# Wider additions of sums, and one more pair of k tiles by seven products, in an encoder block on one core

## The chip, the cores and the metric

The kernel runs on one core of a Trainium2 chip. The metric is the device time of one execution in microseconds (us). A core has TensorE (PE; its weight loads are shown apart as PEld), VectorE (DVE), ScalarE (ACT), GpSimd (POOL) and SyncE (SP). SyncE and GpSimd issue the transfers between the chip's memory and the core's own memory, each on a queue of its own, and sixteen DMA engines carry them out.

## The reference

One layer of a bidirectional encoder for 256 tokens of 2048 features, all in float32:

```python
proj = rmsnorm(h, mix_norm_pre) @ w_in                 # 2048 -> 4640
z, xbc, dt_raw, u = split(proj)
mix = concat([ssd_mixer(z, xbc, dt_raw, ...), pool_mixer(u, ...)]) @ w_out
h = h + rmsnorm(mix, mix_norm_post)
up = rmsnorm(h, ffn_norm_pre) @ w_ffn_up               # 2048 -> 2 x 5632
gate, val = split(up, 2)
ff = (gelu(dwconv_centred(gate, ...)) * val) @ w_ffn_down   # 5632 -> 2048
h = h + rmsnorm(ff, ffn_norm_post)
gate = sigmoid(rmsnorm(h, ple_norm_pre) @ w_ple_gate)  # 2048 -> 2048
h = h + rmsnorm(gate * (p @ w_ple), ple_norm_post)
```

What costs time are the matrix products: w_in, w_out, up, down and the gate. The change touches three of them.

## The kernel before

**Split numbers.** Every product is done three times, in a faster rounded format (fp32r). A factor x is split into hi, x rounded by ScalarE (`split`, line 196, or `hid_split`, line 1369), and lo, the rest x - hi, a subtraction on VectorE (lines 197 and 1370). Then x @ w is hi @ hi + hi @ lo + lo @ hi. So each weight costs ScalarE one pass and VectorE one pass before TensorE can use it. The split weights lie in five buffers (tag `w`); a ScalarE pass waits until TensorE has left the buffer.

**Pairs of k tiles.** In w_out, down and the gate (`token_major`), the columns come in two halves of 1024, and the rows of the weights in pairs of k tiles of 128 rows each. A plain pair is 2 k tiles x 2 token tiles x 2 column blocks of 512 x 3 = 24 matmuls of 512 columns. A pair can instead be done by seven products (`seven_products`, Strassen's scheme in Winograd's form), which is 7 x 3 = 21 matmuls. It needs four sums of blocks of the weights (`block_adds`, line 305) and four sums of blocks of the left factor (`pair_sums`, lines 1202 to 1207, and in `cat_sums` for w_out). Its weights are split in four pieces, named a (512 columns), b, d and c (1024 each), against two pieces of 1024 for a plain pair. d and c are made from the block sums. `combine` puts the products together once per half.

**Where sums are made.** Block sums of down and the gate are mostly made early, in the up stage, and stored: `block_sums` loads 1 MB of weights (`fetch`, tile dnb or gtb), adds (`add`) and stores them in the chip's memory (`store`, on GpSimd's queue, tile dns or gts). A list `which` holds them; the two for the first pairs of down stay in the core's memory. Job number i is placed at up's piece 45 i / 10 + 4, its additions three pieces later. Pairs listed in `dn_here` (15 in the first half; 6 and 13 in the second) make their block sums in down itself, just before the pair. The left factor of down, the hidden activations, has its sums stored in up for the pairs in `dn_stored` (tile hsum, 512 KB each), kept in place for `OWN`, and loaded again by GpSimd (line 1521, tile hd, three buffers).

**Down's second half.** Pairs are numbered 0 to 21; pair u holds the k tiles 2u and 2u + 1. Tiles are named by half and k tile: dn120 is the pair of k = 20 in the second half, that is pair 10. With r ends the name of the weights as loaded (three buffers), with t that of the block sums, with aw to dw that of the split pieces; weights of plain pairs appear as dn1r, dn_0w and dn_1w. `dn_fast` lists the pairs done by seven products. In the second half the plain pairs are 0, 1, 10, 17, 20 and 21. A fast pair with stored block sums loads 768 KB of weights and 1024 KB of sums; a plain pair loads 1024 KB. SyncE's loads for this half are chained in program order (`load`, `IN_ORDER`). The first weights of the gate (tile gtf, 1 MB, `first_raw`) are asked for ahead of pair 13 and aren't chained.

**The order of work.** Up to w_out, and in up, ScalarE, VectorE and SyncE keep the order of the program (`in_order`). In down and the gate a planner orders each engine's instructions when the program is built, by its own costs, within the data's dependencies.

Of the kernel before, what the change touches and what calls it, by code (L numbers as in the profile page):

```python
# [86 lines left out]
def build(nc, a, out):  # L87
    x = a["x"][0]
# [5 lines left out]
    with tile.TileContext(nc) as tc, \  # L94
# [29 lines left out]


        ep = early.enter_context(tc.tile_pool(name="early", bufs=1))
        mhalf = cp.tile([P, 44], F32, name="mhalf")
        nc.gpsimd.memset(mhalf, -0.5)
        ident = cp.tile([P, P], F32, name="ident")
        make_identity(nc, ident)  # L130

# [74 lines left out]
        class Panel:  # L206
# [58 lines left out]
        def block_sums(name, w, c0, k, held):  # L265


            pg = []

            def fetch():  # L270
                r = page(f"{name}b{c0}_{k}")
                pg.append(r)
                load(r, w[c0 // 1024, k // 2])

            def add():
                add_blocks(pg[0])
# [23 lines left out]
        def block_adds(r, t=None):  # L300

            v = r.rearrange("p (b c) -> p b c", b=4)
            s = v if t is None else t.rearrange("p (b c) -> p b c", b=4)
            for n, (i, a, b) in enumerate(((1, v, 0), (0, v, 3), (3, s, 1), (2, s, 3))):
                nc.vector.tensor_add(s[:, i], v[:, i], a[:, b])  # L305
                if n == 1:
                    yield

        def add_blocks(r, t=None):
            for _ in block_adds(r, t):  # L310
                pass
# [182 lines left out]
        for u in range(0, NK, 2):  # L494
            r = [wp.tile([P, 2048], F32, tag="raw", bufs=3, name=f"dtur{u}") if u else r0, page(f"dtur{u + 1}")]
            for j in range(2):
                k = u + j
# [20 lines left out]
            for j in range(2):  # L518
                k = u + j
# [139 lines left out]
                                        1.0 - 2.0 * d, None, op0=ALU.mult)  # L659
            done.add("steps")  # L660

        pth = cp.tile([P, 2, L], F32R, name="pth")
        ptl = cp.tile([P, 2, L], F32R, name="ptl")

        def embedding():

# [372 lines left out]

        sums_got, sums_pages = {}, []  # L1040

        def cat_sums(k):
            if k < 8:
                yield from after(f"yt{k}")
            else:
                yield from after(f"map{(k - 8) // 2}")
            yield from take("mid")
            n = len(sums_got)
            sums_got[k] = None
            if n % 2 == 0:  # L1050
# [6 lines left out]
            a11, a21, a12, a22 = (v[:, i * P:(i + 1) * P] for i in range(4))  # L1057
            s1, s2, s3, s4 = (s[:, i * P:(i + 1) * P] for i in range(4))
            nc.vector.tensor_sub(s1, a22, a21)
            nc.vector.tensor_sub(s3, a11, a21)  # L1060
            nc.vector.tensor_add(s2, s1, a11)
            nc.vector.tensor_sub(s4, a12, s2)
            yield
            nc.scalar.copy(o[:, :512], s[:, :512])
            yield
            nc.vector.tensor_sub(o[:, 512:], s[:, :512], o[:, :512].bitcast(F32))
            give("mid")
            sums_got[k] = {f"s{i + 1}": (o[:, i * P:(i + 1) * P], o[:, 512 + i * P:512 + (i + 1) * P]) for i in range(4)}
# [86 lines left out]
        def turn_over():  # L1155
            go_on()
            next_piece()
            go_on()

        jobs = dict(fill=seg_fill, h=load_h, piled=piled, gate=gate, yturn=y_turn, csum=cat_sums, steps=steps, mix_in=pool_mix, map=pool_map, sums=seg_sums, decays=decays, seg=seg, cb=cb,  # L1160
                    weigh=weigh, turn=xs_turn, far=far, skip=skip, mix=mix, embedding=embedding)

        with in_order():
            for _ in range(AHEAD - 2):
                next_piece()
            for n in range(24):
                slab, i, q = (2, 0, 1)[n // 8], n // 4 % 2, n % 4
# [27 lines left out]
            load(g, src.partition_broadcast(P))  # L1195
            return g

        def pair_sums(name, s, o, a11, a21, a12, a22):


            s1, s2, s3, s4 = (s[:, i * P:(i + 1) * P] for i in range(4))
            nc.vector.tensor_sub(s1, a22, a21)
            nc.vector.tensor_sub(s3, a11, a21)
            nc.vector.tensor_add(s2, s1, a11)
            nc.vector.tensor_sub(s4, a12, s2)  # L1205
            nc.scalar.copy(o[:, :512], s[:, :512])  # L1206
            nc.vector.tensor_sub(o[:, 512:], s[:, :512], o[:, :512].bitcast(F32))
            return sums_in(o)

        def sums_in(o):  # L1210
            return {f"s{i + 1}": (o[:, i * P:(i + 1) * P], o[:, 512 + i * P:512 + (i + 1) * P]) for i in range(4)}

        class Sums:
# [5 lines left out]
            def __call__(self, k):  # L1219
                if k not in self.got:  # L1220
                    n = len(self.got)
                    if n % 2 == 0:
                        self.pages.append(page(f"{self.name}p{k}", F32R))
                    s = mid(f"{self.name}s{k}")
                    c = slice((k % 8) * L, (k % 8 + 2) * L)
                    v = s[:, 512:]
                    nc.vector.tensor_add(v, self.pan.hi[k // 8][:, c].bitcast(F32), self.pan.lo[k // 8][:, c].bitcast(F32))
                    self.got[k] = pair_sums(f"{self.name}{k}", s, self.pages[-1][:, n % 2 * 1024:(n % 2 + 1) * 1024],
                                            *(v[:, i * P:(i + 1) * P] for i in range(4)))
# [110 lines left out]
            h_kept.append(dp.tile([P, D], F32, tag=f"h{t}", bufs=1, name=f"h_kept{t}"))  # L1340
        pl_kept = dp.tile([P, D], F32, tag="pl", bufs=1, name="pl_kept")

        dn_fast, gt_fast = ((1,2,3,4,5,6,7,8,9,10,11,12,13,14,15,16,17,18,19), (2,3,4,5,6,7,8,9,11,12,13,14,15,16,18,19)), ((4, 5, 6), (1, 2, 3))

        dn_here = (15,), (6,13,)
        dn_stored = (2,3,5,7,8,10,11,13,14,16,17,18,19)
# [7 lines left out]
        jobs_at[6].append(lambda: load(pl_kept, pl[0]))  # L1354
        for i, w_ in enumerate(which[2:] + which[:2]):
            fetch, add, store = block_sums(*w_, i >= len(which) - 2)
            n = 45 * i // 10 + 4
            jobs_at[n].append(fetch)
            jobs_at[n + 3].extend((add, store))
        hid, kept = [], {}  # L1360

        def hid_part(k):
            return hid[k // 8][:, (k % 8) * L:(k % 8 + 2) * L]
# [10 lines left out]
            early_hs[k] = hid_split(k)  # L1374

        def hid_sums_of(k, s, o):
            return pair_sums(f"he{k}", s, o, *(hid_part(k)[:, i * P:(i + 1) * P] for i in (2, 3, 0, 1)))

        OWN = (12, 18, 24, 30)
        own, own_pages = {}, []  # L1380
# [13 lines left out]
        def own_sums(k):  # L1394
            own[k] = hid_sums_of(k, sp.tile([P, 512], F32, tag="junk", bufs=1, name=f"hs{k}"), own_place(k))
# [72 lines left out]
        with in_order():  # L1468
# [3 lines left out]
            for n in range(NPIECES):  # L1472
                s, v, i = blocks[n // 4]
# [98 lines left out]
        vg = [page(f"vg{t}") for t in range(2)]  # L1572
        sq = [[], []]

        half_up = cp.tile([P, 1], F32, name="half_up")
        nc.gpsimd.memset(half_up, 0.5)

        def rest_of(o):

            base = EPS * D  # L1580
            for n, q in enumerate(sq[1]):
                m = tiny(f"go1m{n}", 1)
                nc.gpsimd.tensor_scalar(m, q, 1.0, base, op0=ALU.mult, op1=ALU.add)
                base = m
            nc.gpsimd.tensor_tensor(o, m, half_up, op=ALU.pow)

        def finish(t):
            if t:
# [20 lines left out]
        for half in range(2):  # L1609
# [127 lines left out]
```

## Time and profile before

| what | value |
|---|---|
| median of three runs | 1097.18 us (1096.76 to 1097.2) |
| profiled execution | 1096.73 us, span 1095.0 us |
| TensorE busy | 1088.7 us, 99% of the span |
| VectorE busy | 976.5 us, 89% |
| ScalarE busy | 738.2 us, 67% |
| transfers | 367.45 MB, 336 GB/s over the span |
| stages, by first matmul | xbc 52, z 137, w_out 190, up 285, down 777, gate 1000 us |

The span runs from the first to the last instruction; the profiled execution's own time holds a little more around it. A line such as `L305 DVE TENSOR_TENSOR dnb<-dnb 128x512` names the kernel's line, the engine, the operation, the tiles written and read, and the shape. All matmuls have line 123, that of a helper, so they are told apart by tiles: dna, dns, dn0s and dn1s are the accumulators of down, ga and va those of up. In a timeline the columns are start and duration in us, and in square brackets the idle time before and what ended it.

### The profile page before, as it was taken

The page shows a single profiled execution, that of the slowest core. Times are in us where ns is not written, and L with a number is a line of the kernel's source. Part 1 is how long each engine was busy: PE and PEld are TensorE (multiplying, and loading weights), DVE is VectorE, ACT ScalarE, POOL GpSimd, SP SyncE. Part 2 cuts the span into 40 slices and gives each one's busy share as a digit, 9 for nine tenths or more (in the row PEclk, how much of TensorE's full clock was granted, in tenths as well). Part 3 has the DMA queues.
Part 4 walks back from the last instruction along what each step waited for, and adds up shares of the span by engine and source line. Part 5 has one row for each costly group of instructions (what it writes and reads, how often), then busy time and mean ns, then how long its engine had stood idle before and what let it go on. Part 6 is the DMA issues. An engine that isn't in the chain of part 4 may idle for free.

```text
span 1095.0 us, 15720 instructions
## 1 busy us (share of the span) xinstructions
PE 1088.7 (99%) x5766; PEld 937.1 (86%) x5766; DVE 976.5 (89%) x1367; ACT 738.2 (67%) x1109; POOL 100.1 (9%) x163
## 2 busy tenths in 40 slices
PE   9999999999999999999999999999999999999998
PEld 9988888888888888888888888888888888888886
DVE  6678988999879888889889988888999999999997
ACT  6687777566776565565756646657688868786773
POOL 0211111100100000000000000000000000051001
PEclk9999999999999999999999999999999999999999
DMA  9987699587589999989999998999999999996872
GB/s 359 426 250 203 202 278 279 212 317 273 189 346 404 398 402 364 398 345 373 389 364 378 369 386 349 408 357 423 366 409 382 380 346 390 424 390 221 320 278 78
DMA packets 59565, 367.45 MB, mean 336 GB/s; under 512 B 6672, under 2 KB 7696, under 8 KB 24208
## 3 DMA queue, kind: packets, MB, share of 16 engines
q1 hardware_dynamic: 45808, 302.74, 70.5%
q0 software_dynamic: 13536, 63.44, 17.3%
q8 instruction: 45, 0.74, 0.3%
q14 instruction: 32, 0.26, 0.1%
q10 hardware_dynamic: 144, 0.26, 0.1%
HBM read 315.56 MB, written 61.34 MB: 344 GB/s over the span
## 4 chain that ended last, share of the span: by engine, by line
PE 97%; DVE 1%; POOL 1%; ACT 0%; issue 0%; POOLq 0%; DVEq 0%; ACTq 0%
PE ga L123 22%; PE va L123 22%; PE dna L123 11%; PE xbc L123 6%; PE woa L123 5%; PE gt L123 5%; PE dns L123 4%; PE dtu L123 4%; PE z L123 4%; PE dn0s L123 2%; PE dn1s L123 2%; PE ple L123 1%; PE wo1s L123 1%; PE gts L123 1%; PE yd L123 1%; PE pw L123 1%
## 5 line engine op out<-in xcount | busy, mean ns | idle before, releaser
L123 PE MATMUL ga<-wox,ug_0w 128*128 128x512 f32 x704 | 130.8, 337 | 0.0
L123 PE MATMUL ga<-wox,ug_1w 128*128 128x512 f32 x704 | 130.1, 337 | 0.0
L123 PE MATMUL va<-wox,uv_0w 128*128 128x512 f32 x704 | 129.2, 336 | 0.0
L123 PE MATMUL va<-wox,uv_1w 128*128 128x512 f32 x704 | 129.2, 336 | 0.0
L123 PEld LDWEIGHTS ga<-wox,ug_0w 128*128 128x128 f32 x704 | 107.7, 188 | 14.5 <-ACT pl L1289 0.2
L123 PEld LDWEIGHTS ga<-wox,ug_1w 128*128 128x128 f32 x704 | 107.5, 188 | 14.5 <-DVE wox L234 0.2
L123 PEld LDWEIGHTS va<-wox,uv_1w 128*128 128x128 f32 x704 | 107.5, 188 | 14.5
L123 PEld LDWEIGHTS va<-wox,uv_0w 128*128 128x128 f32 x704 | 107.5, 188 | 14.5
L305 DVE TENSOR_TENSOR dnb<-dnb 128x512 f32<-128x512 f32 x128 | 88.3, 690 | 3.0
L283 POOL DMA_DIRECT2D dns<-dnb x30 | 16.1, 536 | 317.4 <-DVE dnb L305 256.2
L1206 ACT CAST he<-he 128x512 fp32r<-128x512 f32 x13 | 8.1, 621 | 42.8 <-DVE he L1205 42.8
L123 PE MATMUL xbc<-hn,xb_1w 128*128 128x512 f32 x192 | 36.5, 338 | 0.0
L123 PE MATMUL xbc<-hn,xb_0w 128*128 128x512 f32 (+1 forms) x192 | 36.4, 340 | 0.0
L123 PEld LDWEIGHTS xbc<-hn,xb_0w 128*128 128x128 f32 x192 | 29.7, 188 | 4.1
L123 PEld LDWEIGHTS xbc<-hn,xb_1w 128*128 128x128 f32 x192 | 29.5, 188 | 4.1 <-issue 0.2
L1369 ACT CAST hs<-hid 128x384 fp32r<-128x384 f32 (+1 forms) x44 | 23.5, 538 | 12.9 <-PE dna L123 12.7
L1449 ACT ACTIVATE fc<-gr,vt 128x256 f32<-128x256 f32 x44 | 26.1, 593 | 8.6 <-DVE gr L1442 8.6
L1521 POOL DMA_DIRECT2D hd<-hsum x24 | 12.7, 529 | 191.0 <-PE dn1s L123 76.3
L123 PE MATMUL dna<-dn_0w,hs 128*128 128x512 f32 x108 | 28.3, 391 | 0.0
L123 PE MATMUL dna<-dn_1w,hs 128*128 128x512 f32 x108 | 28.0, 390 | 0.0
L1370 DVE TENSOR_TENSOR hs<-hid,hs 128x384 fp32r<-128x384 f32 (+1 forms) x44 | 25.5, 582 | 2.1 <-ACT hs L1369 2.1
L1452 DVE TENSOR_TENSOR fc<-fc,ft 128x510 f32<-128x510 f32 x22 | 15.2, 689 | 11.3 <-ACT ft L1450 11.3
(1778 smaller groups left out, 2796.0 us busy)
## 6 DMA issues: line engine op xcount, KB each, us to landing
dnb<-w_down SPq DMA_DIRECT2D x32, 1024.0 KB, 10.4
dns<-dnb POOLq DMA_DIRECT2D x30, 1024.0 KB, 7.0
hd<-hsum POOLq DMA_DIRECT2D x24, 512.0 KB, 8.1
dtur<-w_dtu SPq DMA_DIRECT2D x14, 528.0 KB, 9.6
hsum<-he POOLq DMA_DIRECT2D x13, 512.0 KB, 7.8
gtb<-w_gate SPq DMA_DIRECT2D x6, 1024.0 KB, 10.1
gts<-gtb POOLq DMA_DIRECT2D x6, 1024.0 KB, 9.2
dn1r<-w_down SPq DMA_DIRECT2D x6, 1024.0 KB, 6.8
```

Of the source, the lines that this page charges most:

```text
L123: last["pe"] = ins(nc.tensor.matmul(o, lhsT, rhs, start=start, stop=stop, skip_group_check=True))
L283: nc.gpsimd.dma_start(t, pg[0])
L305: nc.vector.tensor_add(s[:, i], v[:, i], a[:, b])
L1206: nc.scalar.copy(o[:, :512], s[:, :512])
L1369: nc.scalar.copy(t[:, :c1], hid_part(k)[:, :c1])
L1370: nc.vector.tensor_sub(t[:, 512:512 + c1], hid_part(k)[:, :c1], t[:, :c1].bitcast(F32))
L1449: nc.scalar.activation(c[:, f], v[:, f], AF.Identity, bias=vec(V_FCB + 4 * s + 2 * i + f), scale=vec(w + NF))
L1452: nc.vector.tensor_add(c[:, :, 1:], c[:, :, 1:], l[:, :, :L - 1])
L1521: nc.gpsimd.dma_start(o.bitcast(F32), kept[k])
```

## The change

Four things change.

1. In `block_adds` the first two of the four additions of 128 x 512 become one of 128 x 1024, with blocks taken in reversed order and with a stride of three blocks. The third and fourth stay.
2. The four sums of the left factor get one helper, `four_sums`. Its first two subtractions of 128 x 128 become one of 128 x 256, one operand being read twice. It is used in w_out, down and the gate.
3. Pair 10 of down's second half (k = 20) is done by seven products. Its block sums are one more job in up, so the list has 39 jobs instead of 38, and job i is placed at piece 44 i / 10 + 4. Its hidden sums are in `dn_stored` already, for the first half; the second half loads them once more.
4. Some small tiles change size or place: `mhalf` has 32 columns instead of 44, `half_up` 24 instead of 1, and `pth` and `ptl` (the split embedding) are allocated earlier. The work done on them is the same.

```diff
@@ build
-        mhalf = cp.tile([P, 44], F32, name="mhalf")
+        mhalf = cp.tile([P, 32], F32, name="mhalf")
         nc.gpsimd.memset(mhalf, -0.5)
+        pth = cp.tile([P, 2, L], F32R, name="pth")
+        ptl = cp.tile([P, 2, L], F32R, name="ptl")
...
@@ block_adds
-            for n, (i, a, b) in enumerate(((1, v, 0), (0, v, 3), (3, s, 1), (2, s, 3))):
-                nc.vector.tensor_add(s[:, i], v[:, i], a[:, b])
-                if n == 1:
-                    yield
+            nc.vector.tensor_add(s[:, 1::-1], v[:, 1::-1], v[:, 0::3])
+            yield
+            nc.vector.tensor_add(s[:, 3], v[:, 3], s[:, 1])
+            nc.vector.tensor_add(s[:, 2], v[:, 2], s[:, 3])
...
+        def four_sums(s, v, diagonal, a21, a12):
+
+            s, v = (x.rearrange("p (i c) -> p i c", i=4) for x in (s[:, :512], v))
+            nc.vector.tensor_sub(s[:, 2::-2], v[:, diagonal], v[:, a21].unsqueeze(1).to_broadcast([P, 2, P]))
+            nc.vector.tensor_add(s[:, 1], s[:, 0], v[:, diagonal.start])
+            nc.vector.tensor_sub(s[:, 3], v[:, a12], s[:, 1])
...
@@ cat_sums (and the same in pair_sums)
-            nc.vector.tensor_sub(s1, a22, a21)
-            nc.vector.tensor_sub(s3, a11, a21)
-            nc.vector.tensor_add(s2, s1, a11)
-            nc.vector.tensor_sub(s4, a12, s2)
+            four_sums(s, v, slice(0, 4, 3), 1, 2)
...
@@ pairs of down and the gate
-        dn_fast, gt_fast = ((1,2,3,4,5,6,7,8,9,10,11,12,13,14,15,16,17,18,19), (2,3,4,5,6,7,8,9,11,12,13,14,15,16,18,19)), ((4, 5, 6), (1, 2, 3))
+        dn_fast, gt_fast = ((1,2,3,4,5,6,7,8,9,10,11,12,13,14,15,16,17,18,19), (2,3,4,5,6,7,8,9,10,11,12,13,14,15,16,18,19)), ((4, 5, 6), (1, 2, 3))
...
-            n = 45 * i // 10 + 4
+            n = 44 * i // 10 + 4
...
-        half_up = cp.tile([P, 1], F32, name="half_up")
+        half_up = cp.tile([P, 24], F32, name="half_up")
```

More of the change, by code (lines that the diff above doesn't have):

```diff
@@ L660, in steps @@
             done.add("steps")
-        pth = cp.tile([P, 2, L], F32R, name="pth")
-        ptl = cp.tile([P, 2, L], F32R, name="ptl")
         def embedding():
@@ L1056, in cat_sums @@
             nc.vector.tensor_add(v, cat.hi[k // 8][:, c].bitcast(F32), cat.lo[k // 8][:, c].bitcast(F32))
-            a11, a21, a12, a22 = (v[:, i * P:(i + 1) * P] for i in range(4))
-            s1, s2, s3, s4 = (s[:, i * P:(i + 1) * P] for i in range(4))
-            nc.vector.tensor_sub(s1, a22, a21)
-            nc.vector.tensor_sub(s3, a11, a21)
-            nc.vector.tensor_add(s2, s1, a11)
-            nc.vector.tensor_sub(s4, a12, s2)
+            four_sums(s, v, slice(0, 4, 3), 1, 2)
             yield
@@ L1196, in gload, with pair_sums @@
             return g
[L1198 to L1205, printed above, removed]
+        def pair_sums(s, o, v, *places):
+            four_sums(s, v, *places)
             nc.scalar.copy(o[:, :512], s[:, :512])
@@ L1227, in __call__ @@
                     nc.vector.tensor_add(v, self.pan.hi[k // 8][:, c].bitcast(F32), self.pan.lo[k // 8][:, c].bitcast(F32))
-                    self.got[k] = pair_sums(f"{self.name}{k}", s, self.pages[-1][:, n % 2 * 1024:(n % 2 + 1) * 1024],
-                                            *(v[:, i * P:(i + 1) * P] for i in range(4)))
+                    self.got[k] = pair_sums(s, self.pages[-1][:, n % 2 * 1024:(n % 2 + 1) * 1024], v, slice(0, 4, 3), 1, 2)
                 (h1, l1), (h2, l2) = self.pan(k), self.pan(k + 1)
@@ L1376, in hid_sums_of @@
         def hid_sums_of(k, s, o):
-            return pair_sums(f"he{k}", s, o, *(hid_part(k)[:, i * P:(i + 1) * P] for i in (2, 3, 0, 1)))
+            return pair_sums(s, o, hid_part(k), slice(2, 0, -1), 3, 0)
         OWN = (12, 18, 24, 30)
@@ L1584, in rest_of @@
                 base = m
-            nc.gpsimd.tensor_tensor(o, m, half_up, op=ALU.pow)
+            nc.gpsimd.tensor_tensor(o, m, half_up[:, :1], op=ALU.pow)
         def finish(t):
```

## The prediction

> **What bounds the kernel now.** I read the page first, then the chain of waits, then windows over the stretch where the new pair goes, then the timelines of the engines and queues in it.
>
> ```profile
> span 1095.0 us, 15720 instructions
> PE 1088.7 (99%) x5766; PEld 937.1 (86%) x5766; DVE 976.5 (89%) x1367; ACT 738.2 (67%) x1109; POOL 100.1 (9%) x163
> PE 97%; DVE 1%; POOL 1%; ACT 0%; issue 0%; POOLq 0%; DVEq 0%; ACTq 0%
> ```
>
> The profiled execution took 1096.73 us (its span of 1095.0 and 1.73 around it), 0.45 under the median of the runs, 1097.18. TensorE is the chain, so what counts is what else is full where the change touches it. In the chain of waits:
>
> ```profile
> 732.42 22.19 PE ga L123 x128
> 933.19 5.44 PE dna L123 x24
> 939.31 2.04 PE dna L123 x9
> 944.07 2.04 PE dna L123 x9
> 953.67 2.04 PE dna L123 x9
> ```
>
> A half slab of up is 128 matmuls in 22.19 us. In down, the plain pair k = 20 (the one to be changed) is 24 matmuls in 5.44; from 939.31 to 944.07 a pair by seven products, 21 matmuls, takes 4.76. The next two take 9.60 instead of 9.52: TensorE hardly waits. Then windows; the last three columns are granted clock, DMA share and GB/s.
>
> ```profile
> 100.00:200.00 100.00, 100.00 (x521) 84.30 (x520) 92.09 (x143) 71.31 (x143) 11.48 (x17) 1.00 0.80 245
> 500.00:600.00 100.00, 100.00 (x579) 88.12 (x578) 89.56 (x132) 58.51 (x88) 5.85 (x11) 1.00 0.96 375
> 905.32:910.08 4.76, 4.76 (x22) 3.94 (x21) 4.76 (x7) 4.20 (x6) 0.53 (x1) 1.00 0.99 350
> 919.00:944.00 25.00, 25.00 (x112) 20.68 (x111) 23.00 (x26) 18.93 (x24) 1.07 (x3) 1.00 1.01 411
> 924.36:929.12 4.76, 4.76 (x22) 3.94 (x22) 4.76 (x7) 3.72 (x4) 0.53 (x2) 1.00 0.99 373
> 938.64:943.40 4.76, 4.76 (x22) 3.94 (x22) 3.83 (x5) 4.51 (x6) 0.00 (x0) 1.00 1.00 424
> ```
>
> In up VectorE (the third busy time) has 10 of 100 us free. From 919 to 944 TensorE has no idle time, VectorE has 2 of 25 us, and the DMA engines are always busy (share 1.01, 411 GB/s). Three full resources meet where the change adds work to one and bytes to another.
>
> **The change: TensorE.** One pair goes from 24 to 21 matmuls: 5.44 - 4.76 = 0.68 us less. This is all that it can win on the chain directly.
>
> **The change: VectorE.** Its timeline around the plain pair, and at the next pair whose block sums are made in down (k = 26):
>
> ```profile
> 928.91 1.22 DVE L197 TENSOR_TENSOR dn118cw<-dn118t,dn118cw 128x1024 fp32r<-128x1024 f32 x1
> 930.05 1.22 DVE L197 TENSOR_TENSOR dn_0w<-dn1r,dn_0w 128x1024 fp32r<-128x1024 f32 x1
> 944.75 1.29 DVE L305 TENSOR_TENSOR dn126t<-dn126r 128x512 f32<-128x512 f32 x2
> 945.96 0.69 DVE L305 TENSOR_TENSOR dn126t<-dn126r,dn126t 128x512 f32<-128x512 f32 x1
> 946.56 0.69 DVE L197 TENSOR_TENSOR dn126aw<-dn126r,dn126aw 128x512 fp32r<-128x512 f32 x1
> 947.76 1.22 DVE L197 TENSOR_TENSOR dn126bw<-dn126r,dn126bw 128x1024 fp32r<-128x1024 f32 x1
> 948.90 0.56 DVE L1370 TENSOR_TENSOR hs<-hid,hs 128x384 fp32r<-128x384 f32 x1
> 949.37 1.22 DVE L197 TENSOR_TENSOR dn126dw<-dn126t,dn126dw 128x1024 fp32r<-128x1024 f32 x1
> ```
>
> What one instruction costs the engine is the step to the next start: 1.14 for 1024 columns (928.91 to 930.05), 0.60 for 512 (945.96 to 946.56), 0.47 for 384 (948.90 to 949.37). A plain pair is 2 x 1.14 + 0.60 = 2.88; a pair by seven products with stored sums is 0.60 + 3 x 1.14 + 0.47 = 4.49. So k = 20 adds 1.61, and TensorE asks for everything behind it 0.68 sooner: 2.29 us of slack are wanted. From 930.05 to 944.75 VectorE has 14.70 us and works 2.88 (k = 20) + 2 x 4.02 (the weights of k = 22 and 24) + 3 x 0.47 (three hidden splits) = 12.33. It has 2.37 to spare, so VectorE alone just bears it.
>
> The wider block addition: two instructions of 512 columns become one of 1024, 1.20 to 1.14, 0.06 less. No such form with two strided inputs stands in the trace; the bounds are 1.14 and two whole durations of the 512 form, 1.38 (0.18 more). I take the lower, since the nearest row, a two-input subtraction of 1024 columns, has it. The wider 128-column subtractions:
>
> ```profile
> 892.46 0.28 DVE L1202 TENSOR_TENSOR hs<-hid 128x128 f32<-128x128 f32 x1
> 892.66 0.28 DVE L1203 TENSOR_TENSOR hs<-hid 128x128 f32<-128x128 f32 x1
> ```
>
> Two steps of 0.20 become one of 256 columns, between 0.20 and 0.40; some 0.07 less each. Most of these sums lie in up, z and w_out, under matmuls that run on; I count 0 for them, with 0.1 either way.
>
> **The change: up.** One job more: a load and a store of 1 MB each, and 1.14 + 2 x 0.60 = 2.34 us of additions. Against it stand 38 jobs that save 0.06 (2.3 us) and the narrow sums. VectorE's free 10% hides both, and TensorE's 22.19 shows that its weights were never late. The DMA share goes from 0.96 to about 0.97, the spacing of jobs from 4.5 to 4.4 pieces. I count 0. Were that cover gone, it would cost at most the 2 MB at 411 GB/s, 5 us; nothing in the chain over up speaks for it.
>
> **The change: DMA in down.** Here the bill comes. The loads in order, on SyncE's queue and (hd) on GpSimd's:
>
> ```profile
> 918.94 0.33 SPq L152 DMA_DIRECT2D dn1r<-w_down  x1
> 928.75 0.44 SPq L152 DMA_DIRECT2D gtf<-w_gate  x1
> 932.43 0.33 SPq L152 DMA_DIRECT2D dn126r<-w_down  x1
> 928.73 0.53 POOL L1521 DMA_DIRECT2D hd<-hsum  x1 [4.23 <-PE dn1s L123]
> 943.98 0.53 POOL L1521 DMA_DIRECT2D hd<-hsum  x1 [14.73 <-PE dn1s L123]
> DMA to landing us min/median/max: 11.7/11.7/11.7
> DMA to landing us min/median/max: 12.9/12.9/12.9
> 944.22 0.63 ACT L196 CAST dn126aw<-dn126r 128x512 fp32r<-128x512 f32 x1 [0.83 <-DMA dn126r<-w_down]
> 962.41 1.05 ACT L196 CAST gtfh<-gtf 128x1024 fp32r<-128x1024 f32 x1
> dn122r<-w_down SPq DMA_DIRECT2D x1, 768.0 KB, 7.3
> dn1r<-w_down SPq DMA_DIRECT2D x1, 1024.0 KB, 8.6
> hd<-hsum POOLq DMA_DIRECT2D x3, 512.0 KB, 8.3
> ```
>
> dn126r (11.7 from issue to landing) lands at 932.43 + 11.7 = 944.1, behind gtf (12.9) at 928.75 + 12.9 = 941.7: 1 MB in 2.45 us, back to back. It is already just in time: ScalarE waits for it until 944.22, and VectorE's additions start at 944.75. The plain pair's 1024 KB, issued at 918.94, become 768 KB of weights and 1024 KB of stored block sums, 768 KB more on SyncE's queue ahead of dn122r, dn124, gtf and dn126r, which all wait behind it. The stored hidden sums of k = 20 are one more load of 512 KB on GpSimd. These loads are released by the third one before them, so k = 28's, now issued at 928.73, moves to the end of the new pair, about 938, and runs beside gtf and dn126r.
>
> At 411 GB/s, 768 KB (0.786 MB) is 1.9 us and 512 KB (0.524 MB) is 1.3: an upper bound of 3.2. The lower bound is the first alone at 424 GB/s, 1.9, less what the slow window at 924 could still move ((424 - 373) x 4.76 = 0.24 MB, 0.6): 1.3. I take 2.2, as part of the second will be over by then. dn126r then lands at 946.3 and the additions start at 946.4 instead of 944.75: 1.65 late, 1.59 after the wide one.
>
> Is there slack behind it? TensorE at this pair, the window behind it, and a row of the chain that the sum below uses:
>
> ```profile
> 948.66 0.39 PE L123 MATMUL dna<-dn126bw,hs 128*128 128x512 f32 x1
> 944.75:971.90 27.15, 27.15 (x120) 22.27 (x120) 27.15 (x32) 21.98 (x28) 14.31 (x3) 1.00 1.01 418
> 914.56 2.27 PE dna L123 x9
> ```
>
> dn126bw's subtraction begins at 947.76 and needs 1.22, to 948.98; its first matmul is issued at 948.66, while it ends. There is none. From 944.75 to 971.90, past the plain pair k = 34, VectorE has no pause (27.15 of 27.15), so TensorE follows it 1.59 later than now, and the 0.68 it had won is spent in the wait (about 2.3 us in all). What follows k = 34 is as before, shifted.
>
> **Sum.** -0.68 won, +2.27 waited at k = 26, and 0.06 won at each of the two other pairs with sums made in down (k = 30 of the first half, k = 12 of the second, where TensorE waits today: 2.27 for nine matmuls at 914.56 instead of 2.04): about +1.5 us. 1096.73 + 1.5 = 1098.2 for a profiled execution, **1098.6** as a median. With the bounds of the delay, 1.3 to 3.2, the wait leaves +0.6 to +2.5, which is 1097.7 to 1099.6.
>
> **Rivals.**
> - *The bytes find room (about 1096.3).* gtf is first read at 962.41 and isn't chained to the other loads. If the planner puts it behind dn126r, that load comes 2.45 earlier, at 946.3 - 2.45 = 943.9, before VectorE is ready at 944.75 - 0.68 = 944.07. Then all of 0.68 + 3 x 0.06 = 0.86 is won. For it: the load is free to move. Against it: its issue stands right behind dn124's, and nothing in the diff moves it.
> - *The queue runs at its slow rate (about 1100.1, slower by over 0.2%).* At the 350 GB/s of the window at 905, also at share 0.99 and beside a hidden-sums load, 1.31 MB take 3.7 us: dn126r lands at 947.8, +3.1 - 0.1 = +3.0. It decides from a delay of about 2.9 on, where the loss passes 2.2 us. For it: two such windows lie close by. Against it: gtf to dn126r moved 1 MB in 2.45 us, 428 GB/s. [...]
> - *The wide addition is no gain (+0.5).* With 1.38 for it, each of the three pairs made in down costs 0.18 more instead of 0.06 less, 0.7 in all: 1099.3, if the wait at k = 26 stands.
> - *Something before down moves by over 2 us* (another order of instructions in z and w_out, where VectorE is 92% busy, or in the gate): 1094 to 1096. The edits there are five sums and one block addition, so little speaks for it.
>
> **How the numbers follow.** What a measurement of this kernel can tell from no change is about 0.2%, 2.2 us. Forecast 0.57, room 0.19, slow queue 0.12, no gain 0.06, elsewhere 0.06. Faster by over 0.2%: the last and a little of the second, 0.07. Slower: the slow queue, the top of the forecast's range and of the fourth case, 0.19. Within: 0.74. The range runs from just under the first rival to the slow queue: 1096.0 to 1100.2.
>
> **What would show it.** Right: ScalarE and VectorE wait for the DMA of dn126r by 1.5 us or more; dn126r lands near 946.3; TensorE's gaps at k = 26 add up to about 2.3 us, with none at k = 20 to 24; up's half slabs still take 22.19. Wrong: gtf issued behind dn126r; no gap at k = 26; a 1024-column addition far from 1.22 us long; gaps in up.

## The result, and the profile after

The changed kernel takes 1101.1 us (median of 7 runs, 1100.37 to 1102.44) against 1097.2 for the kernel before on the same chip (7 runs, 1096.76 to 1098.16): a ratio of 1.0034, with a 95% interval of 1.0024 to 1.0044. It is slower by 3.9 us, where the prediction had 1098.6 and a range up to 1100.2. The profiled execution took 1102.24 us, 5.5 more than that of before; some of this difference is one of the execution and not of the kernel, as will be seen.

From the page of the changed kernel, engines, the chain's shares and the block additions that are left in up:

```profile
span 1100.5 us, 15662 instructions
PE 1091.4 (99%) x5763; PEld 938.0 (85%) x5763; DVE 975.0 (89%) x1303; ACT 739.6 (67%) x1111; POOL 101.0 (9%) x165
...
PE 89%; DVE 5%; issue 1%; DMA 1%; ACT 1%; POOL 1%; POOLq 0%; DVEq 0%; ACTq 0%
...
L306 DVE TENSOR_TENSOR dnb<-dnb 128x1024 f32<-128x1024 f32 x33 | 40.2, 1218 | 0.3 <-DMA dnb<-w_down 0.3
```

TensorE has its three matmuls less, VectorE has less to do than before (975.0 instead of 976.5), and a wide addition takes the 1.22 us that was assumed. Yet TensorE's share of the chain fell from 97% to 89%: other engines now end last. Where, the chain of waits shows (start, duration, what):

```profile
732.69 22.19 PE ga L123 x128
...
932.58 1.15 DVE dn120bw L199
933.75 15.37 DMA dn126r<-w_down
949.14 1.23 DVE dn126t L306
...
952.75 2.55 PE dna L123 x5
```

Up's half slab still takes 22.19. Then the load of dn126r stands in the chain, and behind it VectorE's additions, before TensorE goes on. The timelines of VectorE, ScalarE and TensorE at this place (in brackets the idle time before, and what ended it):

```profile
949.14 1.23 DVE L306 TENSOR_TENSOR dn126t<-dn126r 128x1024 f32<-128x1024 f32 x1 [1.85 <-DMA dn126r<-w_down]
...
952.62 0.68 DVE L309 TENSOR_TENSOR dn126t<-dn126r,dn126t 128x512 f32<-128x512 f32 x1
...
949.19 0.62 ACT L198 CAST dn126aw<-dn126r 128x512 fp32r<-128x512 f32 x1 [2.50 <-DMA dn126r<-w_down]
...
953.41 1.04 ACT L198 CAST dn126dw<-dn126t 128x1024 fp32r<-128x1024 f32 x1 [2.66 <-DVE dn126t L309]
...
953.77 1.05 PE L123 MATMUL dna<-dn126bw,hd 128*128 128x512 f32 x2
954.63 0.68 PE L123 MATMUL dna<-dn126dw,hs 128*128 128x512 f32 x1
```

Three things are to be seen. Both engines wait for dn126r, by 1.85 and 2.50 us. The rounding of dn126d starts 953.41 - 949.14 = 4.27 us after the additions began. Before, they began at 944.75 (in the prediction), and VectorE's last addition and ScalarE's rounding were

```profile
947.16 0.69 DVE L305 TENSOR_TENSOR dn126t<-dn126r,dn126t 128x512 f32<-128x512 f32 x1
...
947.96 1.06 ACT L196 CAST dn126dw<-dn126t 128x1024 fp32r<-128x1024 f32 x1 [1.75 <-DVE dn126t L305]
```

which is 947.96 - 944.75 = 3.21. And two matmuls of 512 columns take 954.63 - 953.77 = 0.86 us, 0.43 each, where they took 2.04 / 9 = 0.227 before. Windows over the same place explain the last (the third column from the end is the granted clock):

```profile
948.00:950.00 2.00, 1.00 (x5) 0.52 (x3) 0.86 (x1) 0.81 (x2) 0.00 (x0) 1.00 1.00 418
950.00:952.00 2.00, 1.55 (x5) 0.72 (x5) 2.00 (x4) 0.76 (x1) 0.00 (x0) 1.00 1.03 428
952.00:954.00 2.00, 1.25 (x3) 1.05 (x4) 1.30 (x2) 0.59 (x1) 0.00 (x0) 0.65 1.02 428
954.00:956.00 2.00, 2.00 (x5) 1.10 (x5) 1.51 (x2) 2.00 (x4) 0.00 (x0) 0.50 1.01 414
956.00:958.00 2.00, 2.00 (x10) 1.64 (x9) 2.00 (x3) 2.00 (x3) 0.00 (x0) 1.00 1.02 409
```

After two windows with TensorE partly idle, its clock was halved for 3.4 us: (1 - 0.65) / 0.5 x 2 = 1.4 us of the third window and all of the fourth.

Not all of the time is lost at k = 26. SyncE's queue is a clock of progress: each load is released by the work a few pairs earlier. Before:

```profile
749.66 0.42 SPq L152 DMA_DIRECT2D dnb<-w_down  x1
...
763.34 0.33 SPq L152 DMA_DIRECT2D dn06t<-dns  x1
...
833.07 0.33 SPq L152 DMA_DIRECT2D dn030r<-w_down  x1
...
898.50 0.33 SPq L152 DMA_DIRECT2D dn112r<-w_down  x1
```

and after, with two rows of ScalarE:

```profile
761.46 0.48 SPq L154 DMA_DIRECT2D dnb<-w_down  x1
...
768.86 0.38 SPq L154 DMA_DIRECT2D dn06t<-dns  x1
...
833.34 0.33 SPq L154 DMA_DIRECT2D dn030r<-w_down  x1
...
899.96 0.33 SPq L154 DMA_DIRECT2D dn112r<-w_down  x1
...
844.73 0.62 ACT L198 CAST dn030aw<-dn030r 128x512 fp32r<-128x512 f32 x1 [0.32 <-DMA dn030r<-w_down]
...
850.08 1.05 ACT L198 CAST dn030dw<-dn030t 128x1024 fp32r<-128x1024 f32 x1 [3.08 <-DVE dn030t L309]
```

At dn030r (the pair k = 30 of the first half) the changed kernel is 0.27 us behind, at dn112r 1.46: 1.2 us go in the first half of down, where only up's jobs and the form of the addition differ. The last job's load (dnb) is issued at 761.46 instead of 749.66, and down's first stored sums (dn06t) behind it at 768.86 instead of 763.34. Tile dn030r took this long from issue to landing, first before, then after:

```profile
DMA to landing us min/median/max: 8.6/8.6/8.6
```

```profile
DMA to landing us min/median/max: 11.3/11.3/11.3
```

It landed at 833.07 + 8.6 = 841.7 before and at 833.34 + 11.3 = 844.6 after, where ScalarE then waited for it.

So there were three theories for the loss, beside the prediction's own:

- **LOADS** (the prediction's): the new pair's bytes make dn126r late.
- **ORDER**: the wide addition (1.23 us) gives its first result later than the first narrow one (0.69) did, so the planner puts other work between it and the additions that need it; the last one ends later. (The order is in the traces; why the planner chose it is inferred from it.)
- **FETCH**: with one job more, the last fetch comes after two loads of down instead of ahead of them, and all stored sums of the first half come one place later.

A fourth, **CLOCK**, came with the runs. Below, an execution kept the clock if its mean granted clock was 0.999 or more.

### The profile page after: what moved, and what is told of

Its sections match the earlier page's. It is cut to its first block, busy times and chain, and to the rows that moved or that the text cites. A ratio compares the mean times of both kernels' runs of the same rounds, so it can differ in the third digit from the quotient of the medians.

```text
span 1100.5 us, 15662 instructions
## 1 busy us (share of the span) xinstructions
PE 1091.4 (99%) x5763; PEld 938.0 (85%) x5763; DVE 975.0 (89%) x1303; ACT 739.6 (67%) x1111; POOL 101.0 (9%) x165
## 4 chain that ended last, share of the span: by engine, by line
PE 89%; DVE 5%; issue 1%; DMA 1%; ACT 1%; POOL 1%; POOLq 0%; DVEq 0%; ACTq 0%
PE ga L123 22%; PE va L123 22%; PE dna L123 7%; PE xbc L123 6%; PE woa L123 5%; PE gt L123 5%; PE dtu L123 4%; PE z L123 4%; PE dns L123 3%; PE dn0s L123 2%; DMA dn126r<-w_down 1%; PE dn1s L123 1%; PE wo1s L123 1%; PE gts L123 1%; PE ple L123 1%
## 5 line engine op out<-in xcount | busy, mean ns | idle before, releaser
L123 PEld LDWEIGHTS va<-wox,uv_0w 128*128 128x128 f32 x704 | 107.6, 188 | 14.4
L123 PEld LDWEIGHTS va<-wox,uv_1w 128*128 128x128 f32 x704 | 107.6, 188 | 14.4
L306 DVE TENSOR_TENSOR dnb<-dnb 128x1024 f32<-128x1024 f32 x33 | 40.2, 1218 | 0.3 <-DMA dnb<-w_down 0.3
L123 PE MATMUL dna<-dn_1w,hs 128*128 128x512 f32 x96 | 25.1, 390 | 0.0
L423 ACT COPY hid<-va 128x256 f32<-128x256 f32 x44 | 15.2, 371 | 13.5 <-PE va L123 13.5
```

The lines of the kernel that those rows point to most:

```text
L123: last["pe"] = ins(nc.tensor.matmul(o, lhsT, rhs, start=start, stop=stop, skip_group_check=True))
L306: nc.vector.tensor_add(s[:, 1::-1], v[:, 1::-1], v[:, 0::3])
L423: nc.scalar.copy(o[:, f * L:(f + 1) * L], acc[f][:, L:])
```

## The experiments

Each kernel ran beside the kernel before on the same chip. The medians of the latter lie between 1096.88 and 1097.19 us, 1097.19 beside the first experiment.

### The change without its pair

```diff
-... (2,3,4,5,6,7,8,9,10,11,12,13,14,15,16,18,19)) ...
+... (2,3,4,5,6,7,8,9,11,12,13,14,15,16,18,19)) ...
-            n = 44 * i // 10 + 4
+            n = 45 * i // 10 + 4
```

> The changed kernel without its new pair: k = 20 of down's second half is plain again and the jobs of up are spaced as before, so only the wider additions and the moved small tiles are left. Theory LOADS (the bytes of the new pair make dn126r late, and that is all): dn126r lands near 944.1 us as in the kernel before, no gap of TensorE over 0.5 us at k = 26, median about 1097.0 (1096.7 to 1097.4). Theory ORDER (the wide addition makes the program place the third and fourth block addition of k = 26 each one place later on VectorE, behind the weights a and b, so that ScalarE's rounding of dn126d starts 4.27 us after the additions begin instead of 3.21): about 1.06 us lost at k = 26 even with dn126r on time, median about 1098.2 (1097.8 to 1098.6).

Measured: 1098.74 us, ratio 1.0015 (1.0006 to 1.0024). No new bytes, no new pair, and still 1.55 us slower: ORDER, a little beyond its range. Its VectorE and ScalarE at k = 26:

```profile
945.13 1.23 DVE L306 TENSOR_TENSOR dn126t<-dn126r 128x1024 f32<-128x1024 f32 x1
946.27 0.69 DVE L199 TENSOR_TENSOR dn126aw<-dn126r,dn126aw 128x512 fp32r<-128x512 f32 x1
946.88 0.68 DVE L308 TENSOR_TENSOR dn126t<-dn126r,dn126t 128x512 f32<-128x512 f32 x1
947.48 1.22 DVE L199 TENSOR_TENSOR dn126bw<-dn126r,dn126bw 128x1024 fp32r<-128x1024 f32 x1
948.61 0.68 DVE L309 TENSOR_TENSOR dn126t<-dn126r,dn126t 128x512 f32<-128x512 f32 x1
...
949.41 1.05 ACT L198 CAST dn126dw<-dn126t 128x1024 fp32r<-128x1024 f32 x1 [2.22 <-DVE dn126t L309]
```

Wide addition, split a, third addition, split b, fourth addition: 945.13 to 949.41 is 4.28 us. The kernel before did all but the last addition first, then split a, and then the last one.

### Narrow additions where they are made in down

```diff
-            nc.vector.tensor_add(s[:, 1::-1], v[:, 1::-1], v[:, 0::3])
+            if t is None:
+                nc.vector.tensor_add(s[:, 1::-1], v[:, 1::-1], v[:, 0::3])
+            else:
+                nc.vector.tensor_add(s[:, 1], v[:, 1], v[:, 0])
+                nc.vector.tensor_add(s[:, 0], v[:, 0], v[:, 3])
             yield
```

Here t is given only for the three pairs whose sums are made in down. First on the changed kernel:

> The changed kernel, with the block additions of the three pairs that are made in down (k = 30 of the first half, 12 and 26 of the second) in four narrow steps again; up's jobs stay wide. Theory LOADS: dn126r still lands near 949 us and the additions wait for it; the time stays within 0.4 us of the changed kernel, 1100.7 to 1101.3. Theory ORDER: ScalarE's rounding of dn126d starts 3.2 us after the additions begin instead of 4.27; 1.06 us come back at k = 26 and up to as much at k = 30 of the first half, median 1099.0 to 1100.0.

Measured: 1100.27 us, ratio 1.003 (1.002 to 1.004), but the 12 executions lie from 1098.39 to 1105.24: eight kept the clock (median 1099.85), four did not (1101.02 to 1101.8). In its profile the rounding of dn126d starts 951.64 - 948.43 = 3.21 us after the additions, as before the change. The time lies between the two theories' ranges, and is no verdict by itself. Then on the change without its pair:

> The changed kernel without its new pair (jobs spaced as before) and with narrow block additions at the three pairs made in down: what is left of the change is the wide additions of the jobs in up and at the gate, the wider 128-column sums, and the moved small tiles. ORDER: the 1.5 us that the wider additions cost without the pair go, median 1097.1 (1096.8 to 1097.4), the gaps at 950 and 998 us too. If the wider 128-column sums or the moved tiles cost it, the time stays at 1098.2 to 1098.8.

Measured: 1096.91 us, ratio 0.9998 (0.9989 to 1.0007): the same as before. Only these additions differ from the first experiment, so they cost 1098.74 - 1096.91 = 1.83 us there (1.6 if each is set against the kernel before that ran beside it), and the wide additions in up, the wider 128-column sums and the moved tiles cost nothing that can be measured. VectorE's first addition and ScalarE at k = 26:

```profile
945.79 0.69 DVE L309 TENSOR_TENSOR dn126t<-dn126r 128x512 f32<-128x512 f32 x1 [1.03 <-DMA dn126r<-w_down]
...
949.00 1.05 ACT L198 CAST dn126dw<-dn126t 128x1024 fp32r<-128x1024 f32 x1 [1.15 <-DVE dn126t L313]
```

949.00 - 945.79 = 3.21, the time of the kernel before. That 1.06 us is not all of the 1.83: near the end of down the chain of the kernel with wide additions runs over VectorE and GpSimd up to TensorE's transposes (tile dnxt):

```profile
989.96 0.71 DVE dna L366
...
997.80 0.76 DVE hb L1272
998.61 0.87 PE dnxt L444 x6
```

With the narrow ones TensorE itself is the chain there:

```profile
989.86 5.09 PE dna L123 x21
```

The price rests on the medians. The two profiled executions took 1098.22 and 1097.71 us, only 0.5 apart, since in the second dn126r landed late (13.4 us after its issue, against 12.5). In the first, TensorE's pauses (here and below the step from one start of a matmul to the next, less 0.227 us a matmul) are longer than in the profile of before by about 0.5 us in the first half of down, 0.9 at k = 26 and 0.7 from 960 to 1000 us.

### The last job's fetch four pieces sooner

```diff
-            n = 44 * i // 10 + 4
+            n = 43 * i // 10 + 4
```

> The changed kernel with the jobs of up spaced by 4.3 pieces instead of 4.4, so that the last one fetches its weights some four pieces sooner. Theory FETCH (in the changed kernel the last job's fetch is issued at 761.46 us instead of 749.66 and takes a page and a place ahead of down's first stored sums, so that each load of the first half of down is issued one slot later and dn030r lands at 844.63 instead of 841.67): dn030r lands near 842 again, the gaps at k = 30 of the first half and those at 881 and 887 us go, about 1.2 us, median 1099.6 to 1100.2. Theory ORDER (the gaps at k = 30 come from the order of its additions and not from the load): the time stays within 0.4 us of the changed kernel, 1100.7 to 1101.3, unless the order at k = 30 changes with it.

Measured: 1100.21 us, ratio 1.0027 (1.0018 to 1.0037), 0.9 less than the changed kernel (in executions that kept the clock 1100.0 against 1100.6). dn030r again took as long as before the change:

```profile
DMA to landing us min/median/max: 8.7/8.7/8.7
```

and the first half of down runs through. FETCH holds in the trace; its size, 0.6 to 0.9 us instead of 1.2, is uncertain, as the intervals of the two kernels overlap. The order of the additions at k = 30 went back too, with the earlier load, probably since the planner lays that pair out by when it expects the load to land; the two are not told apart at this pair.

### The gate's first weights behind dn130

```diff
-... at={13: first_raw, ...
+... at={16: first_raw, ...
```

> The changed kernel with the load of the gate's first weights (gtf, 1 MB) issued three pairs later, behind those of dn126, dn128 and dn130; nothing else moves. Theory LOADS: dn126r lands 1 MB earlier, 2.45 us at the rate between those two loads, so near 946.6 us; TensorE's gaps at k = 26 shrink by about that, median 1098.4 to 1099.0. Theory ORDER alone (the load is late but hidden behind VectorE): the same as the changed kernel, 1100.8 to 1101.3. If the late gtf then holds up the gate's first weights, a new gap appears behind 962 us.

Measured: 1099.09 us, ratio 1.0016 (1.0007 to 1.0025), 2.0 less than the changed kernel (1.5 less than its executions that kept the clock) and 0.1 above the expected range; no execution lost the clock. Issued at 933.8, dn126r took

```profile
DMA to landing us min/median/max: 10.3/10.3/10.3
```

so it landed at 944.1, as in the kernel before and 5.0 us earlier than in the changed kernel, more than the 2.45 of gtf's megabyte. But ORDER's part stayed,

```profile
949.82 1.05 ACT L198 CAST dn126dw<-dn126t 128x1024 fp32r<-128x1024 f32 x1 [3.04 <-DVE dn126t L309]
```

and a new gap of 0.5 us stood at k = 34 (968 to 969 us).

### The pair alone

On the kernel before:

```diff
-... (2,3,4,5,6,7,8,9,11,12,13,14,15,16,18,19)) ...
+... (2,3,4,5,6,7,8,9,10,11,12,13,14,15,16,18,19)) ...
-            n = 45 * i // 10 + 4
+            n = 44 * i // 10 + 4
```

> The kernel before with only the new pair: k = 20 of down's second half by seven products, its job in up, jobs spaced by 4.4 pieces; all additions stay narrow and the small tiles where they were. LOADS (dn126r late behind the new bytes: 2.3 to 2.6 us waited at k = 26, 0.68 won) and FETCH (the later last fetch: 0.9 us at k = 30 of the first half and behind it) together give 1097.2 + 1.7 to 1.9 + 0.9, so 1099.8 (1099.4 to 1100.3). If ORDER, the wide addition, were the main part of the loss, this kernel would be within 0.5 us of the one before: 1096.7 to 1097.7.

Measured: 1099.68 us, ratio 1.003 (1.002 to 1.004): inside the range expected for LOADS and FETCH together, and far from what ORDER as the main part would give (1096.7 to 1097.7). That the number fits so well is partly luck: three of 11 executions lost the clock (1101.22 to 1101.98), which the expectation did not contain, and the median of the other eight is 1099.3, just below its range.

### Only LOADS left

The changed kernel with the narrow additions in down and the spacing of 4.3, both edits as above.

> The changed kernel with two parts undone at once: narrow block additions at the three pairs made in down, and jobs spaced by 4.3 pieces. If LOADS, ORDER and FETCH are all there is, only LOADS is left, which is what the prediction summed: dn126r lands 2.2 to 2.7 us later than in the kernel before, TensorE waits 2.3 to 2.6 us at k = 26, median 1098.7 (1098.3 to 1099.3). Above 1099.5, a further cause is open.

Measured: 1100.54 us, ratio 1.0032 (1.0022 to 1.0041), above the 1099.5 that would leave a cause open. The executions fall into two groups: four kept the clock, 1098.53 to 1098.91; seven did not, 1100.44 to 1103.62. The first group is where LOADS has it. In the profile, which is of the second group:

```profile
950.00:952.00 2.00, 0.97 (x3) 0.54 (x4) 1.95 (x3) 1.50 (x2) 0.00 (x0) 0.84 1.04 435
952.00:954.00 2.00, 2.00 (x6) 1.52 (x6) 2.00 (x3) 1.96 (x3) 0.00 (x0) 0.50 1.00 422
```

So the halved clock is most of what was open.

### Work in place of the wait

```diff
...
             t31 = split(f"{name}c", t[:, :1024], 1024)
+            if name == "dn126":
+                for n in range(10):
+                    mm(alt[n % 4], a_["a11"][0], keep24["c"][0][:, :512], False, False)
+            keep24["c"] = t31
```

> The kernel with narrow additions in down and jobs spaced by 4.3 pieces, with ten more matmuls of 512 columns (2.27 us) put ahead of k = 26's first product, so that TensorE works while it would wait for dn126r. They add a product of already split tiles to the running sums, so what is computed is no longer the reference. Theory CLOCK (the waits at k = 26, 2.8 us of idle time within 4 us, are what halves the granted clock for 3 us in about half of the executions, 1.6 to 3.5 us more): no execution shows a clock under 0.999, all lie near those that kept the clock, 1098.5 to 1099.3, median 1098.9, though there are ten matmuls more. If the halving has nothing to do with the wait: median 1100.5 or more, still split in two groups.

Measured: 1099.6 us (1098.72 to 1100.03), ratio 1.002 (1.0011 to 1.0029). All 11 executions kept the clock, and with ten matmuls more the median is 0.9 lower. Its windows, with TensorE at work until the load came:

```profile
950.00:952.00 2.00, 1.50 (x6) 0.63 (x4) 2.00 (x4) 0.48 (x1) 0.00 (x0) 1.00 1.03 432
952.00:954.00 2.00, 1.39 (x6) 1.17 (x7) 1.95 (x3) 2.00 (x4) 0.00 (x0) 1.00 1.03 433
```

TensorE still paused for 1.1 us in these two windows (1.50 and 1.39 busy of 2), and the median is 0.3 above the expected range. The clock was kept although dn126r took 15.7 us to land here, the longest of all, so a late load by itself did not halve it. CLOCK, that TensorE's idle time did, agrees with this; no other cause was tried.

### Everything undone but the pair

The same two edits, and gtf issued right behind dn126r (`at={14: first_raw,`), or behind dn130 (`at={16: first_raw,`).

> As the kernel with narrow additions in down and jobs spaced by 4.3 pieces, and gtf's load issued right behind dn126r instead of ahead of it. LOADS: dn126r lands when VectorE is ready for it (before 945), no gap over 0.5 us at k = 26, and the 0.68 us of the pair are won: median 1096.5 (1096.2 to 1097.0). If the loads behind it (dn128 and on) are late in its place, or the gate's first weights hold up k = 34, a new gap of 0.5 to 1 us and 1097.0 to 1097.6.

> Narrow additions in down, jobs spaced by 4.3 pieces, and gtf's load three pairs later, behind those of dn130. No load that k = 26 to 30 need stands behind gtf: no gap over 0.5 us from 945 to 960 us. The load of the plain pair k = 34 and VectorE's split of gtf then meet at 968: a gap of 0.6 to 0.9 us there, as in the kernel with only the late gtf. Together 0.68 won and 0.6 to 0.9 lost: median 1097.0 (1096.7 to 1097.6), the same as before. A median under 1096.6 would say that the pair is worth having; one over 1098, that bytes which the pair adds must be paid at whatever load stands last.

Measured: 1098.26 us, ratio 1.001 (1.0001 to 1.0018), and 1098.34, ratio 1.0012 (1.0003 to 1.0021). Both are above the ranges expected: the 0.68 us of the pair are not won. The second is over 1098, which was named beforehand as the sign that the pair's bytes are paid at whatever load stands last. With gtf last, the load of the plain pair k = 34 is what TensorE waits for, in the chain

```profile
952.90 13.12 DMA dn1r<-w_down
...
968.69 3.49 PE dna L123 x14
```

with a gap of 1.3 us ahead of 968.69. Bytes moved out of the way of one load made another late. With gtf right behind dn126r there is a gap of 0.45 at 968, and two of 0.4 at k = 28, which are not of a late load:

```profile
951.38 0.51 ACT L1369 CAST hs<-hid 128x384 fp32r<-128x384 f32 x1 [1.70 <-PE dna L123]
951.79 0.61 ACT L198 CAST dn128aw<-dn128r 128x512 fp32r<-128x512 f32 x1
```

dn128r had landed by 949.6; its rounding stood behind the split of the hidden activations, which waited for TensorE to leave its buffer. And with the first split of gtf one pair later:

```diff
-17: lambda: first(0)
+18: lambda: first(0)
```

> The same, and the first split of the gate's first weights one pair later (after the plain pair k = 34 instead of ahead of it). If VectorE's order at k = 34 costs what the gap at 969 us in the kernel with the late gtf shows (0.6 us), this is 0.3 to 0.6 faster than the kernel with gtf right behind dn126r: 1096.1 (1095.8 to 1096.6). If that gap came from the late gtf alone, both are the same within 0.2 us.

Measured: 1102.88 us, ratio 1.0049 (1.0037 to 1.0062), a clear miss: 4.6 slower than with that split where it was. The planner gave the end of down another order, and the same kind of wait came with it, now with the rounding of dn136d behind it:

```profile
974.27 0.52 ACT L1369 CAST hs<-hid 128x384 fp32r<-128x384 f32 x1 [3.02 <-PE dna L123]
```

### The pair without its bytes

On the kernel with only LOADS left, k = 20 takes the sums of k = 18 that are still in the core's memory.

```diff
+            if name == "dn120":
+                r = raw(f"{name}r", w[c0 // 1024, k0 // 2])
+                t = keep18["t"]
-            if (stage, c0, k0) in sums_:
+            elif (stage, c0, k0) in sums_:
...
+            if k == 20 and 'dn120' in keep18:
+                d = own[18]
-            if k in own:
+            elif k in own:
```

> The kernel with narrow additions in down and jobs spaced by 4.3 pieces, without the new pair's extra loads in down: k = 20 takes the block sums of k = 18 that still lie in SBUF and k = 18's hidden sums, in place of its own (so what is computed is no longer the reference), and its weights come as one load of 1 MB, as before the change. Every operation of TensorE, VectorE and ScalarE is that of the pair by seven products; the bytes are those of the plain pair. Theory LOADS (the pair is paid for in bytes alone): dn126r lands near 944 us, no gap over 0.5 us at k = 26 and none behind, 0.68 us won: median 1096.3 (1096.0 to 1096.8), 2 us less than the best group of the kernel with the bytes. Theory VECTOR (VectorE's 2.29 us more are what TensorE waits for, in whichever place): it falls to no less than 1097.5.

Measured: 1097.32 us, ratio 1.0011 (1.0000 to 1.0022); ten of 12 executions lie from 1096.45 to 1098.42, two at 1102. It lies between the theories. The bytes cost 1.5 us (1098.86, the median of the kept group with them, less 1097.32). But the 0.68 us are not won without them either. VectorE at k = 26:

```profile
942.70 1.22 DVE L199 TENSOR_TENSOR dn124cw<-dn124t,dn124cw 128x1024 fp32r<-128x1024 f32 x1
945.38 0.69 DVE L310 TENSOR_TENSOR dn126t<-dn126r 128x512 f32<-128x512 f32 x1 [1.46 <-DMA dn126r<-w_down]
```

VectorE, with all the pair's work done, is free at 943.9 and waits 1.46 us: it is not short. The load is late again, with the bytes of the kernel before. From issue to landing dn126r took 11.7, 12.5, 13.4 and 13.5 us in the four profiles with the plain pair's bytes and gtf ahead (the kernel before, the two without the pair, this one), and 14.3, 14.4, 14.6, 15.4 and 15.7 in five with the pair's (alone, fetch early, only LOADS, the changed kernel, work in place of the wait). The profile of before was the earliest of its group. This spread is not one of the order of loads: the kernel without its pair and with narrow additions issues every load from 904 to 933 us, on both queues, within 0.1 us of where the kernel before does, and its dn126r took 13.4 us against 11.7. Whether executions or chips differ, no run here tells apart.

## Why the prediction was right or wrong

Three steps failed: the wide addition counted as a small gain, up counted as 0, and a wait of TensorE counted at its own length alone. The path that the forecast followed, the late load of dn126r, was there, and about of the size in its sum.

**TensorE, 0.68 less.** The three matmuls are gone, and the prediction had their gain spent in a wait. So it was; even with the bytes for free nothing of it could be measured.

**VectorE just bears the pair.** Right, and only just: VectorE has no idle time from 916 to 940 us in the changed kernel, and the chain runs over it there. No gap stood at k = 20 to 24, and with the bytes taken away VectorE waited for the load and not TensorE for VectorE.

**The wide addition, 0.06 less each.** The price was right (1.22 us) and the step was wrong. It costed the instruction where it stood and assumed that its neighbours keep their places. In down the planner orders them; the two additions behind the wide one need its result, so other work went ahead of them, and the fourth addition, on which the split of d waits, came 1.06 us later after the first. That cost 1.6 to 1.8 us without the pair and 1.1 with it, where 0.2 were to be won. The rival of a wide addition without a gain had the right sign, but another mechanism and only 0.7 us.

**The narrower sums and the moved tiles, 0.** Right: the kernel with these and the wide additions in up alone is at 0.9998 of the one before.

**Up, 0.** Right for what it looked at (22.19 per half slab) and wrong beyond: it counted the spacing of the jobs and the work, and not that the last of 39 jobs stands later in SyncE's queue than the last of 38 did, behind two of down's loads. This cost 0.6 to 0.9 us in the first half of down, where the forecast had no step at all.

**DMA in down, 2.2 us on dn126r.** The mechanism was right in each part: gtf stayed ahead, the hidden-sums load moved (to 939.64 on GpSimd's queue, 938 was said), ScalarE and VectorE waited for dn126r. But dn126r landed at 949.1 and not near 946.3, and TensorE's pauses at k = 26 came to 2.9 us instead of 2.3. Of the 5.0 us that it landed later than before, 1.3 come from its later issue (933.75 instead of 932.43), which the prediction held fixed: the load waits until VectorE has done dn120bw, and the kernel was 1.46 behind since the first half. The rest, from issue to landing, was 15.4 - 11.7 = 3.7 in the two profiles compared, beyond the upper bound of 3.2; between the means of the profiles of each kind, 14.9 and 12.8, it is 2.1. So the term was about right in size, but it was added to one execution whose load landed early. With the other two causes undone, the four of 11 executions that kept the clock take 1098.5 to 1098.9, and the forecast's sum was 1098.6.

**The clock.** It was in no step of the forecast. A wait of 2.3 us was costed as 2.3 us. With only LOADS left, 7 of 11 executions were 1.6 to 4.8 us longer than the median of those that kept the clock; in the changed kernel it was three of 7 (1101.76 to 1102.44, the others 1100.37 to 1101.1), which lifts its median by 0.5. The clock does not explain every long execution: five in four of the kernels tried (1102.72 without the pair, 1105.24 with narrow additions, 1104.51 with the pair alone, 1102.13 and 1102.36 without its bytes) kept it and were 4 to 5.4 us above the median of their group, while none of the 104 of the kernel before that ran beside them exceeds 1098.71. No trace shows one of the five, and their cause stays open.

**The sum.** In executions that kept the clock: 1096.9 with the additions narrow in down and no pair, 1098.9 with the pair, 1100.0 with the wide additions too, 1100.6 with the later fetch. With the clock, 1101.1. The parts measured alone (1.8 for ORDER) are larger than in this sum (1.1), probably since waits at the same place hide each other.

**The rivals.** That the bytes find room was tried and failed: with gtf right behind dn126r the time is 1098.3, not 1096.3, with gaps at k = 28 and k = 34 that are not of late loads. With gtf behind dn130 it is 1098.3 too: the DMA engines are full there (share 1.02, 424 GB/s from 925 to 975 us), and the wait moves on to the load of k = 34. The slow queue named nearly the time that came, and a delay of 3.7 like that of the two profiles, but by luck, as its reason did not hold: 418 to 428 GB/s were moved while dn126r was waited for.

**The range.** It took the rivals as alternatives. Three losses happened together, in places that do not exclude each other, and the range had no term for a sum of several small mistakes.

## What to carry to other kernels

The wide addition (a step of 1.14 us, where the two narrow ones took 1.20) was not only shorter: its first result came later, 1.22 us after its start instead of 0.69, and the planner let what needs that result slide back, by 1.06 us. Keep the narrow form on the path that is just in time and use the wide one where there is cover. When a list of jobs gets one more entry, follow the last entry past the end of its stage, and compare more than one execution before trusting the landing time of a load that is just in time (11.7 to 13.5 us here, with the same bytes ahead).

## What the runs showed of the hardware

The granted clock of TensorE fell to 0.50 behind pauses of which the longest was about 1.2 us. In the changed kernel it did five matmuls between 948.7 and 952.75 us, with pauses of about 1.2, 0.7, 0.1 and 0.9 us, and then ran at 0.43 us a matmul instead of 0.227; the granted clock was halved for 3.4 us. In eight of the 13 kernels tried no execution lost the clock; in the other five, the changed kernel among them, between 1 of 9 and 7 of 11 did. Seven of them have windows around k = 26. TensorE's idle time there was, among the five, 2.2 us in the changed kernel and 2.0 with the last job's fetch four pieces sooner (944 to 956 us), and 1.9 with only LOADS left (946 to 958). Among the eight it was 1.2 without the pair's bytes (917 to 967), 1.1 with work in place of the wait (946 to 958), and 0.2 with gtf behind dn130, in the changed kernel (944 to 956) and with everything undone but the pair (917 to 967). With 2.0 us idle the profiled execution kept a clock of 1.00, with 1.9 another fell to 0.50. How much idle time it takes, and why only some executions lose the clock, no run here shows.

The other surprise was the spread of one load: in four kernels with the same bytes ahead of it, dn126r took between 11.7 and 13.5 us to land, and 11.7 and 13.4 in two that issue it, and every load from 904 us on ahead of it, within 0.1 us of each other.
